# Routing of the last two tiles from rows without norm, in a hybrid decoder layer on one Trainium2 core

## The chip, the cores and the metric

One core of a Trainium2 chip runs the whole layer in one launch. The metric is the device time of one execution in microseconds, as a median over runs. Engines are named as the profile names them: PE (TensorE), PEld (its weight loads), DVE (VectorE), ACT (ScalarE), POOL (GpSimd) and SP (the queue that issues most DMAs).

## The reference, cut to what matters

```python
x = layer_norm(DN_ALPHA * x + merged @ w_out, ln1_g, ln1_b)          # 1024 tokens, 1024 wide, f32
moe = hierarchical_moe(x, ...)
x = layer_norm(DN_ALPHA * x + moe, ln2_g, ln2_b)

def layer_norm(x, g, b):
    mu = jnp.mean(xf, axis=-1, keepdims=True)
    var = jnp.mean(jnp.square(xf - mu), axis=-1, keepdims=True)
    return (xf - mu) * lax.rsqrt(var + LN_EPS) * g + b

def hierarchical_moe(x, w_rg, b_rg, w_re, b_re, ...):
    glog = xt @ w_rg + b_rg                       # 4 groups: the best one is taken
    elog = xt @ w_re + b_re                       # 32 experts: the best two of the group
    weights = gw * softmax(top_v)
    ...                                           # SwiGLU of the two experts, weighted sum
```

Ahead of this stand the input projection, a gated linear recurrence, sliding-window attention and the mixing of their two branches into `merged`.

## The kernel before

Four stages follow each other: attention with its projections, the recurrence, **mixing** (branches, `w_out`, first norm, routing) and the **experts** with the last norm. The change touches mixing alone.

Products that must be exact are three matmuls of split operands (`mm3`, lines 100 to 104). `mixing` runs 32 main steps, each in two halves, so 64 **ticks**. For each half of the tokens, 8 steps `branch(half, jt)` make `merged`, and 8 steps `project(b, i, c)` make half `c` (512 columns) of the `w_out` rows of tile `i` (128 tokens). Tile 6 is steps 28 and 29, tile 7 steps 30 and 31: its last half is ticks 62 and 63. A tick issues its half of the main step on PE, then what `self.at(tick, ...)` put on its list (line 879), then the step's `post`, then the late stages (line 885). The block stands in `all_order()`: each engine, SP's queue included, takes its instructions in exactly this order, and waits in it.

`post` of `project` (lines 815 to 822) adds the residual on DVE (L818) and its statistics (L819); after the second half `stats` (L896, L678, and the power on POOL, L679) gives mean and inverse deviation, and `norm` (line 826) runs two ticks later: `scale` is four DVE instructions per tile (L903, L904), then `store` (L842) writes the tile twice to DRAM, to `x1d` for the gathers and to `zd`, the running sum. The router works on batches of two tiles, at the tick distances in `BATCHES` (line 915): `turn` transposes a normed tile on PE (L931) and copies it (L933); `logits` multiplies by `w_r` (L940, copy with bias L941); `choose` (late) transposes the logits back (L956) and finds the best group and experts on DVE (L946 to L988); `place` (late) ranks the tokens with matmuls (L996, L998) and makes slot rows (L1002 to L1018); `enter` (late) adds them to the table of slots (L1025). All logits and ranks lie in one PSUM bank, `pa`. `warm` (line 110) issues matmuls whose result nobody reads, `WARM` (line 117) says after which ticks.

`slots` (line 1030) turns the table into row indices (L1038), starts the first two gathers of expert rows from `x1d` on POOL (L1064), splits three weight pieces and counts the fullest expert (L1050). `overflow` loads that count on every engine and branches past a loop (L1354, L1355). Then `moe` walks 384 weight **pieces** of 512 KB: 12 per expert.

Weights come by `fetch` (line 1093) on SP's queue: up to `NRAW` = 29 pieces before the experts begin (10 of them in ticks 48 to 60, 4 each after ticks 62 and 63, then 2 per tick), one per piece used after that. They live in a ring of 36 buffers (`q4`), and fetch n waits until fetch n-8 has landed (lines 1106 and 1111). At the end `final` reads all of `zd` back (L1287), behind the last weights on the same queue, and the last norm runs on ACT, DVE and POOL.

Of the kernel before, what the change touches and what calls it, by code (L numbers as in the profile page):

```python
# [5 lines left out]
F32 = mybir.dt.float32  # L6
# [54 lines left out]
class Builder:  # L61
# [679 lines left out]
    def mixing(self):  # L741
# [4 lines left out]
        self.wr = self.tile([128, 8, 36], F32, "wr", 1)  # L746
        self.br = self.tile([36, 1], F32, "br", 1)

        def constants():
# [53 lines left out]
        def project(b, i, c):  # L803
# [11 lines left out]
            def post():  # L815
                t, st = u[i]
                cs = slice(c * 512, c * 512 + 512)
                nc.vector.scalar_tensor_tensor(t[:, cs], xr[i][:, cs], ALPHA, ps, op0=ALU.mult, op1=ALU.add)  # L818
                nc.vector.bn_stats(st[:, c], t[:, cs])  # L819
                if c == 1:  # L820
                    mv = self.stats(st, LN_EPS)
                    self.at(2 * b + 2, lambda: norm(2 * b + 2, i, t, mv), True)

            return post

        def norm(b, i, t, mv):
            for c in range(2):
                self.scale(t, mv, g1, b1, c)
            self.at(b + 2 * (i < 7), lambda: store(i, t))
            batch = next(g for g in self.BATCHES if i in g[0])  # L830
            if i == batch[0][0]:
                self.batch = self.router(batch[0])
            for n, d in enumerate(batch[1]):
                fn = self.batch[n]
                if n < 2:
                    self.at(b + d, lambda fn=fn: fn(i, t))
                elif i == batch[0][-1]:
                    self.late_stages.setdefault(b + d, []).append(fn)
# [53 lines left out]

# [21 lines left out]

    BATCHES = ((0, 1), (4, 5, 6, 10, 14)), ((2, 3), (4, 5, 6, 10, 14)), ((4, 5), (2, 3, 4, 6, 7)), ((6, 7), (1, 2, 2, 3, 4))

    def router(self, batch):
# [7 lines left out]

        def turn(i, x1):
            V["xT", i] = []
            for j in range(2):
# [3 lines left out]
                xT = self.tile([128, 4, 128], F32, "rxT", 2)  # L932
                nc.scalar.copy(xT, ps)  # L933
                V["xT", i].append(xT)

        def logits(i, _):
            lg = self.pa[0:36, 0:128]
            for j, xT in enumerate(V.pop(("xT", i))):
                for k in range(4):
                    nc.tensor.matmul(lg, self.wr[:, 4 * j + k], xT[:, k], start=j + k == 0, stop=j == 1 and k == 3)  # L940
            nc.scalar.activation(lT[:, i - batch[0]], lg, AF.Identity, bias=self.br)  # L941

        def first_max(vals, w, nm, ix):

            mx = t((n, 1), nm + "m")
            vec.tensor_reduce(mx, vals, axis=AX.X, op=ALU.max)  # L946
            c = t((n, w), nm + "c")
            for k in range(n):
                vec.scalar_tensor_tensor(c[:, k], vals[:, k], mx[:, k], low[:, 0:w], op0=ALU.is_ge, op1=ALU.mult)
            vec.tensor_reduce(ix, c, axis=AX.X, op=ALU.min)  # L950
            return mx

        def choose():
            l = self.pa[:, 128:128 + 36 * n].rearrange("p (n c) -> p n c", n=n)
            for k in range(n):
                nc.tensor.transpose(l[:, k], lT[:, k], self.c("ident")[0:36, 0:36])  # L956
            gl, el = l[:, :, 0:4], l[:, :, 4:36]
            gi = t((n, 1), "gi")
            gm = first_max(gl, 4, "g", gi)
            em, ge, gs, d = t((n, 32), "em"), t((n, 4), "ge"), t((n, 1), "gs"), t((n, 1), "dd")  # L960
            for k in range(n):
                vec.tensor_scalar(em[:, k], self.c("group"), gi[:, k], -3.0e38, op0=ALU.not_equal, op1=ALU.mult)
            vec.tensor_sub(ge, gl, gm.to_broadcast([128, n, 4]))
            nc.scalar.activation(ge, ge, AF.Exp)
            vec.tensor_add(em, em, el)
            eid = self.eid[:, batch[0]:batch[0] + n]
            oh = t((n, 2, 32), "oh")
            ms = []
            for j in range(2):
                ms.append(first_max(em, 32, "ab"[j], eid[:, :, j:j + 1]))  # L970
                for k in range(n):
                    vec.tensor_scalar(oh[:, k, j], low, eid[:, k, j:j + 1], None, op0=ALU.is_equal)
                for k in range(n if j == 0 else 0):
                    vec.scalar_tensor_tensor(em[:, k], oh[:, k, 0], -3.0e38, em[:, k], op0=ALU.mult, op1=ALU.add)
            asg = t((n, 32), "asg")
# [3 lines left out]
            sums = [self.asum]  # L979
            for k in range(n):  # L980
# [8 lines left out]
            V["r"] = asg, oh, sums, gs, d  # L989

# [470 lines left out]
def arrays(inputs):  # L1461
# [11 lines left out]
        "ln1_g": f["ln1_g"][0],  # L1473
        "ln1_b": f["ln1_b"][0],
        "w_r": np.concatenate([f["router_group_w"][0], f["router_expert_w"][0]], axis=1),
        "b_r": np.concatenate([f["router_group_b"][0], f["router_expert_b"][0]]),
# [21 lines left out]
```

## Time and profile before

| | before |
|---|---|
| median of 3 runs | 1424.0 us (1423.0 to 1429.07) |
| the profiled execution | 1423.78 us |
| its span, first to last instruction | 1421.9 us |
| PE busy | 1359.1 us, 96% |
| DVE, ACT, POOL busy | 1058.2, 792.3, 239.6 us |
| DMA moved | 327.68 MB, mean 230 GB/s |

The span begins at 0 in all views. PE is busy for most of it, but with 122 instructions of `warm` among it, and the experts begin only after the routing of the last tile: the first transposes of gathered rows stand at 788.47, the last product with `w_out` starts before 763.9. The mean granted clock of TensorE is 0.986.

### The profile page before, as it was taken

The page shows a single profiled execution, that of the slowest core. Times are in us where ns is not written, and L with a number is a line of the kernel's source. Part 1 is how long each engine was busy: PE and PEld are TensorE (multiplying, and loading weights), DVE is VectorE, ACT ScalarE, POOL GpSimd, SP SyncE. Part 2 cuts the span into 40 slices and gives each one's busy share as a digit, 9 for nine tenths or more (in the row PEclk, how much of TensorE's full clock was granted, in tenths as well). Part 3 has the DMA queues.
Part 4 walks back from the last instruction along what each step waited for, and adds up shares of the span by engine and source line. Part 5 has one row for each costly group of instructions (what it writes and reads, how often), then busy time and mean ns, then how long its engine had stood idle before and what let it go on. Part 6 is the DMA issues. An engine that isn't in the chain of part 4 may idle for free. (4 is left out here: it accounts for less than half of the span.)

```text
span 1421.9 us, 20450 instructions
## 1 busy us (share of the span) xinstructions
PE 1359.1 (96%) x7162; PEld 1128.3 (79%) x7162; DVE 1058.2 (74%) x1654; ACT 792.3 (56%) x1282; POOL 239.6 (17%) x160
## 2 busy tenths in 40 slices
PE   7999999999999999999998999999999999999844
PEld 5888899988888888788787888888888888888721
DVE  4268977876666764857747889999999999999635
ACT  4367555434444442412201778888888888888533
POOL 0001221210010000410001112222222222222123
PEclk9999999999999999999999999999999999999967
DMA  6124223253334323774557899999999999999972
GB/s 254 56 89 156 88 92 105 67 173 116 126 108 136 111 88 103 240 252 137 174 195 277 314 361 369 370 359 349 360 349 359 357 359 360 360 359 361 370 264 95
DMA packets 142554, 327.68 MB, mean 230 GB/s; under 512 B 18614, under 2 KB 59702, under 8 KB 142448
## 3 DMA queue, kind: packets, MB, share of 16 engines
q1 hardware_dynamic: 132800, 308.78, 60.4%
q0 software_dynamic: 9648, 17.57, 4.8%
q8 instruction: 57, 0.93, 0.3%
q14 instruction: 49, 0.40, 0.1%
HBM read 291.43 MB, written 52.43 MB: 242 GB/s over the span
## 5 line engine op out<-in xcount | busy, mean ns | idle before, releaser
L98 DVE TENSOR_TENSOR el<-er,eh 128x1024 fp32r<-128x1024 f32 x368 | 436.5, 1221 | 53.7 <-ACT eh L97 38.1
L97 ACT CAST eh<-er 128x1024 fp32r<-128x1024 f32 x368 | 368.9, 1053 | 100.6 <-PE mm L103 83.5
L102 PE MATMUL mm<-xh,wh 128*128 128x512 f32 x480 | 198.3, 413 | 8.3 <-ACT wh L97 7.3
L102 PE MATMUL mm<-eh,xh 128*128 128x512 f32 x496 | 196.4, 396 | 0.0
L103 PE MATMUL mm<-el,xh 128*128 128x512 f32 x496 | 196.2, 395 | 0.0
L104 PE MATMUL mm<-eh,xl 128*128 128x512 f32 x496 | 196.1, 395 | 0.0
L103 PE MATMUL mm<-xl,wh 128*128 128x512 f32 x480 | 188.4, 393 | 0.8 <-DVE xl L98 0.8
L104 PE MATMUL mm<-xh,wl 128*128 128x512 f32 x480 | 189.0, 394 | 0.0
L104 PEld LDWEIGHTS mm<-eh,xl 128*128 128x128 f32 x496 | 93.2, 188 | 22.6
L103 PEld LDWEIGHTS mm<-el,xh 128*128 128x128 f32 x496 | 93.2, 188 | 22.3
L102 PEld LDWEIGHTS mm<-eh,xh 128*128 128x128 f32 x496 | 93.2, 188 | 22.3
L102 PEld LDWEIGHTS mm<-xh,wh 128*128 128x128 f32 x480 | 91.1, 190 | 24.2 <-ACT wh L97 7.3
L104 PEld LDWEIGHTS mm<-xh,wl 128*128 128x128 f32 x480 | 90.6, 189 | 20.6 <-DVE wl L98 0.8
L1064 POOL DMA_INDIRECT xg<-x1d,gi x32 | 58.1, 1814 | 279.3 <-PE pb L1127 236.3
L103 PEld LDWEIGHTS mm<-xl,wh 128*128 128x128 f32 x480 | 91.1, 190 | 16.0 <-DVE xl L98 1.4
L102 PE MATMUL mm<-eh,hth 128*128 128x512 f32 x240 | 100.2, 418 | 0.0
L1068 POOL DMA_INDIRECT zd<-y,gi x29 | 69.9, 2411 | 156.5 <-ACT y L1218 156.5
L104 PE MATMUL mm<-eh,htl 128*128 128x512 f32 x240 | 94.8, 395 | 0.0
L103 PE MATMUL mm<-el,hth 128*128 128x512 f32 x240 | 94.8, 395 | 0.0
L102 PE MATMUL mm<-wh,xh 128*128 128x256 f32 x256 | 73.1, 285 | 0.0
L104 PE MATMUL mm<-wh,xl 128*128 128x256 f32 x256 | 72.4, 283 | 0.0
L103 PE MATMUL mm<-wl,xh 128*128 128x256 f32 x256 | 72.4, 283 | 0.0
(257 smaller groups left out, 2566.6 us busy)
## 6 DMA issues: line engine op xcount, KB each, us to landing
er<-w_g SPq DMA_DIRECT2D x128, 512.0 KB, 12.5
er<-w_u SPq DMA_DIRECT2D x128, 512.0 KB, 12.5
er<-w_d SPq DMA_DIRECT2D x128, 512.0 KB, 12.0
wr<-w_in SPq DMA_DIRECT2D x38, 512.0 KB, 4.4
gated<-st SPq DMA_DIRECT2D x32, 256.0 KB, 2.1
st<-gated SPq DMA_DIRECT2D x32, 256.0 KB, 2.7
xr<-xt SPq DMA_DIRECT2D x8, 512.0 KB, 7.6
wab<-w_a SPq DMA_DIRECT2D x16, 256.0 KB, 3.7
```

The source lines that it names most:

```text
L97: self.nc.scalar.copy(hi, src)
L98: (eng or self.nc.vector).tensor_sub(lo, src, hi.bitcast(F32))
L102: mm(out, lh, rh, start=start, stop=False)
L103: mm(out, lh, rl, start=False, stop=False)
L104: mm(out, ll, rh, start=False, stop=stop)
L1064: self.nc.gpsimd.indirect_dma_start(to, None, rows, bass.IndirectOffsetOnAxis(ap=self.column(self.gi, e), axis=0), bounds_check=T - 1, oob ...
L1068: self.nc.gpsimd.indirect_dma_start(self.zd, bass.IndirectOffsetOnAxis(ap=idx, axis=0), y, None, bounds_check=T - 1, oob_is_err=False, com ...
```

## The change

- `fold`, at tick 20, makes router weights that take rows without norm: `w_r` times the norm's gain, less its column mean, in `gwr`; and `shift`, the norm's bias through `w_r` plus `b_r`. It is DVE work with one matmul between (its column sums). Two small loads are new.
- Tiles 6 and 7 go through `raw` instead of `norm`. A half tile is transposed as soon as its own half of `w_out` is there, so the first half of tile 7 is transposed and multiplied inside ticks 62 and 63. The inverse deviation and the shift come in at the start of `choose`, in one DVE instruction (`l2`).
- Tile 6 is chosen alone at tick 62, tile 7 alone at the end; `place` and `enter` still take both.
- Tile 6 keeps its norm on DVE; that of tile 7 is one ACT instruction and four on POOL, and its `store` follows in `raw`.
- The batch of tiles 4 and 5 is one tick earlier throughout (`enter` now at tick 62, ahead of the last half of `w_out`).
- 8 fetches are issued in tick 63 before its `post`; the other 11 follow the loop, behind the `store` of tile 7. Fillers: 3, 14 and 7, in `raw`.

```diff
-    WARM = {63: 11, 65: 5, 66: 14, 67: 5}
...
         def constants():
...
+            nc.sync.dma_start(gb, self.a["ln1_gb"])
+            self.shift = self.tile([128, 36], F32, "wshift", 1)
+            nc.sync.dma_start(self.shift, self.a["b_r"].partition_broadcast(128))
+
+        def fold():
+            vec = nc.vector
+            self.gwr = self.tile([128, 8, 36], F32, "gwr", 1)
+            work = self.tile([128, 512], F32, "hh", 2)
+            bwr = work[:, 0:288].rearrange("p (k c) -> p k c", k=8)
+            sums = work[:, 288:360].rearrange("p (j c) -> p j c", j=2)
+            for j, w in enumerate((self.gwr, bwr)):
+                vec.tensor_mul(w, self.wr, gb[:, j, :, None].to_broadcast([128, 8, 36]))
+                vec.tensor_reduce(sums[:, j], w.rearrange("p k c -> p c k"), axis=AX.X, op=ALU.add)
+            ps = self.pa[:, 0:72]
+            nc.tensor.matmul(ps, self.c("ones"), work[:, 288:360], start=True, stop=True)
+            for k in range(8):
+                vec.scalar_tensor_tensor(self.gwr[:, k], ps[:, 0:36], -1.0 / D, self.gwr[:, k], op0=ALU.mult, op1=ALU.add)
+            vec.tensor_add(self.shift, ps[:, 36:72], self.shift)
...
-                if c == 1:
+                if i >= 6:
+                    raw(2 * b + 2, i, t, st, c)
+                elif c == 1:
...
+        def raw(b, i, t, st, c):
+            if i == 6 and c == 0:
+                self.batch = self.router((6, 7))
+            turn, logits, choose, place, enter = self.batch
+            if c == 0:
+                self.at(b, lambda: turn(i, t, (0,)), True)
+                if i == 7:
+                    self.at(b + 1, lambda: logits(i, (0,), self.gwr))
+                return
+            if i == 6:
+                self.at(b, lambda: turn(i, t, (1,)), True)
+                mv = self.stats(st, LN_EPS)
+                self.at(b + 1, lambda: logits(i, (0, 1), self.gwr), True)
+                self.at(b + 1, lambda: [self.scale(t, mv, g1, b1, c) for c in range(2)])
+                self.at(b + 2, lambda: choose(0, 1, mv))
+                self.at(b + 3, lambda: store(i, t), True)
+                return
+            turn(i, t, (1,))
+            mv = self.stats(st, LN_EPS)
+            nm = self.tile([128, 1], F32, "lnm", 1)
+            nc.vector.scalar_tensor_tensor(nm, mv[:, 0:1], -1.0, mv[:, 1:2], op0=ALU.mult, op1=ALU.mult)
+            self.warm(3)
+            logits(i, (1,), self.gwr)
+            nc.scalar.activation(t, t, AF.Identity, scale=mv[:, 1:2], bias=nm)
+            for c in range(2):
+                cs = slice(c * 512, c * 512 + 512)
+                nc.gpsimd.tensor_mul(t[:, cs], t[:, cs], g1[:, cs])
+                nc.gpsimd.tensor_add(t[:, cs], t[:, cs], b1[:, cs])
+            choose(1, 2, mv)
+            self.warm(14)
+            place()
+            store(i, t)
+            self.warm(7)
+            enter()
...
+        self.at(20, fold)
...
+            if tick == 2 * len(main) - 1:
+                for _ in range(8):
+                    self.fetch(True)
             if post:
                 post()
...
-            self.warm(self.WARM.get(tick, 0))
             tick += 1
-            if tick >= 2 * len(main) - 1:
-                for _ in range(4 if tick < 2 * len(main) + 1 else 2):
-                    self.fetch(True)
+        for _ in range(self.NRAW):
+            self.fetch(True)
...
-    BATCHES = ((0, 1), (4, 5, 6, 10, 14)), ((2, 3), (4, 5, 6, 10, 14)), ((4, 5), (2, 3, 4, 6, 7)), ((6, 7), (1, 2, 2, 3, 4))
+    BATCHES = ((0, 1), (4, 5, 6, 10, 14)), ((2, 3), (4, 5, 6, 10, 14)), ((4, 5), (1, 2, 3, 5, 6))
...
-        def choose():
+        def choose(k0=0, k1=n, mv=None):
...
+            if mv is not None:
+                l2 = t((1, 36), "l2")
+                vec.scalar_tensor_tensor(l2[:, 0], l[:, 0], mv[:, 1:2], self.shift, op0=ALU.mult, op1=ALU.add)
+                l = l2
```

`turn` and `logits` get the halves to work on, `choose` and `first_max` the number of tiles.

## Rows read from the trace of the kernel before

**Rows 1.** Busy time by engine of one stretch of the experts, clock, DMA share, GB/s.
```profile
1000.00:1300.00 300.00, 300.00 (x1391) 244.36 (x1391) 272.47 (x267) 246.22 (x301) 72.36 (x34) 1.00 0.99 358
```
**Rows 2.** SP's waits from 1000 to 1200: us in total, times, longest.
```profile
SPq L1105 <- DMA er<-w_u: 53.1, 43, 3.4
```
**Rows 3.** Timeline at the end of the experts: start, us, what [idle before <-releaser].
```profile
1369.69 16.62 PE L1165 MATMUL mm<-er,xh 128*128 128x512 f32 x32 [23.13 <-ACT xh L1136]
1366.50 1.06 ACT L1296 ACTIVATE w<-z 128x1024 f32<-128x1024 f32 x1 [25.57 <-DMA z<-zd]
```
**Rows 4.** Timeline at tick 20, PE and DVE.
```profile
616.57 0.39 PE L104 MATMUL mm<-h,ml 128*128 128x512 f32 x1
618.68 0.75 DVE L904 SCALAR_TENSOR_TENSOR u<-u,lmv,ln_b 128x512 f32<-128x512 f32 x1
```
**Rows 5.** Timeline, DVE: an instruction over 64 columns.
```profile
774.88 0.22 DVE L965 TENSOR_TENSOR rem<-rem,pa 128x64 f32<-128x64 f32 x1
```
**Rows 6.** PE after a pause at the end: its timeline row, and the clock of 5 us.
```profile
1395.10 0.80 PE L1149 MATMUL pb<-const,hh 128*128 128x128 f32 x4 [3.64 <-DVE fv L678]
...
1395.00:1400.00 5.00, 4.90 (x11) 2.46 (x12) 4.19 (x8) 1.86 (x5) 2.90 (x2) 0.66 0.49 197
```
**Rows 7.** Timeline, PE in the last ticks.
```profile
745.77 1.94 PE L940 MATMUL pa<-rxT,wr 128*36 128x128 f32 x16
759.94 0.41 PE L996 MATMUL pa<-rasg,const 128*128 128x32 f32 x2 [0.51 <-ACT rlT L941]
```
**Rows 8.** Timeline, DVE from tile 6's second half to the row indices.
```profile
745.88 0.69 DVE L818 SCALAR_TENSOR_TENSOR u<-xr,mm 128x512 f32<-128x512 f32 x1 [4.92 <-PE mm L104]
751.04 0.17 DVE L946 TENSOR_REDUCE rgm<-pa 128x2 f32<-128x8 f32 x1
756.16 0.68 DVE L818 SCALAR_TENSOR_TENSOR u<-xr,mm 128x512 f32<-128x512 f32 x1
763.91 0.69 DVE L818 SCALAR_TENSOR_TENSOR u<-xr,mm 128x512 f32<-128x512 f32 x1 [0.74 <-PE mm L104]
768.30 0.75 DVE L904 SCALAR_TENSOR_TENSOR u<-u,lmv,ln_b 128x512 f32<-128x512 f32 x1
773.68 0.17 DVE L946 TENSOR_REDUCE rgm<-pa 128x2 f32<-128x8 f32 x1 [4.63 <-PE pa L956]
778.79 0.41 DVE L1002 TENSOR_SCALAR rpay<-roh,const 128x64 f32<-128x64 f32 x2
780.95 0.87 DVE L1018 TENSOR_SCALAR rat<-const,rank 128x128 f32<-128x128 f32 x4
782.43 0.19 DVE L1038 TENSOR_SCALAR gi<-tb 128x32 int32<-128x32 f32 x1 [0.61 <-PE tb L1025]
```
**Rows 9.** Timeline, POOL, and a DVE instruction that starts beside it.
```profile
765.90 0.91 POOL L679 TENSOR_TENSOR lmv<-lmv,mhalf 128x1 f32<-128x1 f32 x1 [17.12 <-DVE lmv L678]
579.40 2.40 POOL L98 TENSOR_TENSOR l<-wo,h 128x1024 fp32r<-128x1024 f32 x1 [3.94 <-ACT h L97]
580.10 2.24 DVE L797 TENSOR_TENSOR st<-st,st 128x512 f32<-128x512 f32 x1
```
**Rows 10.** SP's timeline, and its longest wait in the branch.
```profile
769.08 0.33 SPq L842 DMA_DIRECT2D x1d<-u  x1
791.39 3.65 SPq L1102 DMA_DIRECT2D er<-w_d  x4
...
SPq L1355 <- SPq L1355: 3.7, 1, 3.7
```
**Rows 11.** DMA from 784 to 796, GB/s in 40 slices of 0.3 us.
```profile
GB/s 423 382 423 423 396 382 301 259 233 164 110 109 138 68 123 164 68 27 68 55 41 0 27 14 55 110 68 68 218 273 355 396 355 369 300 300 328 273 300 300
```
**Rows 12.** Timeline of the first gather and its reader; all gathers' time to landing.
```profile
783.51 1.46 POOL L1064 DMA_INDIRECT xg<-x1d,gi  x1 [14.90 <-DVE tw L1039]
788.47 1.07 PE L1127 MATMUL pb<-const,xg 128*128 128x128 f32 x8 [1.33 <-DMA xg<-x1d,gi]
...
DMA to landing us min/median/max: 4.3/8.1/9.7
```

More of the change, by code (lines that the diff above doesn't have):

```diff
@@ L747, in mixing @@
         self.br = self.tile([36, 1], F32, "br", 1)
+        gb = self.tile([128, 2, 8], F32, "gb", 1)
         def constants():
@@ L828, in norm @@
                 self.scale(t, mv, g1, b1, c)
-            self.at(b + 2 * (i < 7), lambda: store(i, t))
+            self.at(b + 2, lambda: store(i, t))
             batch = next(g for g in self.BATCHES if i in g[0])
@@ L924, in router, with turn @@
         lT = self.tile([36, n, 128], F32, "rlT", 1)
-        def turn(i, x1):
-            V["xT", i] = []
-            for j in range(2):
+        def turn(i, x1, js=(0, 1)):
+            for j in js:
                 ps = self.bank("pb", (128, 4, 128))
@@ L931, in turn, with logits, first_max @@
                     nc.tensor.transpose(ps[:, k], x1[:, (4 * j + k) * 128:(4 * j + k + 1) * 128], self.c("ident"))
[L932 to L936, printed above, removed]
+                V["xT", i, j] = self.tile([128, 4, 128], F32, "rxT", 2)
+                nc.scalar.copy(V["xT", i, j], ps)
+        def logits(i, js=(0, 1), w=None):
             lg = self.pa[0:36, 0:128]
-            for j, xT in enumerate(V.pop(("xT", i))):
+            for j in js:
+                xT = V.pop(("xT", i, j))
                 for k in range(4):
[L940 to L945, printed above, removed]
+                    nc.tensor.matmul(lg, (self.wr if w is None else w)[:, 4 * j + k], xT[:, k], start=j + k == 0, stop=j == 1 and k == 3)
+            if js[-1] == 1:
+                if w is None:
+                    nc.scalar.activation(lT[:, i - batch[0]], lg, AF.Identity, bias=self.br)
+                else:
+                    nc.scalar.copy(lT[:, i - batch[0]], lg)
+        def first_max(vals, m, w, nm, ix):
+            mx = t((n, 1), nm + "m")[:, 0:m]
             vec.tensor_reduce(mx, vals, axis=AX.X, op=ALU.max)
-            c = t((n, w), nm + "c")
-            for k in range(n):
+            c = t((n, w), nm + "c")[:, 0:m]
+            for k in range(m):
                 vec.scalar_tensor_tensor(c[:, k], vals[:, k], mx[:, k], low[:, 0:w], op0=ALU.is_ge, op1=ALU.mult)
@@ L951, in first_max @@
             return mx
-        def choose():
+        def choose(k0=0, k1=n, mv=None):
+            if k0 == 0:
+                V["r"] = t((n, 32), "asg"), t((n, 2, 32), "oh"), [self.asum], t((n, 1), "gs"), t((n, 1), "dd")
+            m, ks = k1 - k0, slice(k0, k1)
             l = self.pa[:, 128:128 + 36 * n].rearrange("p (n c) -> p n c", n=n)
-            for k in range(n):
+            for k in range(k0, k1):
                 nc.tensor.transpose(l[:, k], lT[:, k], self.c("ident")[0:36, 0:36])
+            l = l[:, ks]
+            if mv is not None:
+                l2 = t((1, 36), "l2")
+                vec.scalar_tensor_tensor(l2[:, 0], l[:, 0], mv[:, 1:2], self.shift, op0=ALU.mult, op1=ALU.add)
+                l = l2
+            asg, oh, sums, gs, d = V["r"]
+            asg, oh, gs, d = asg[:, ks], oh[:, ks], gs[:, ks], d[:, ks]
@@ L957, in choose @@
             gl, el = l[:, :, 0:4], l[:, :, 4:36]
[L958 to L961, printed above, removed]
+            gi = t((n, 1), "gi")[:, 0:m]
+            gm = first_max(gl, m, 4, "g", gi)
+            em, ge = t((n, 32), "em")[:, 0:m], t((n, 4), "ge")[:, 0:m]
+            for k in range(m):
                 vec.tensor_scalar(em[:, k], self.c("group"), gi[:, k], -3.0e38, op0=ALU.not_equal, op1=ALU.mult)
-            vec.tensor_sub(ge, gl, gm.to_broadcast([128, n, 4]))
+            vec.tensor_sub(ge, gl, gm.to_broadcast([128, m, 4]))
@@ L964, in choose @@
             nc.scalar.activation(ge, ge, AF.Exp)
             vec.tensor_add(em, em, el)
-            eid = self.eid[:, batch[0]:batch[0] + n]
-            oh = t((n, 2, 32), "oh")
+            eid = self.eid[:, batch[k0]:batch[k0] + m]
             ms = []
             for j in range(2):
-                ms.append(first_max(em, 32, "ab"[j], eid[:, :, j:j + 1]))
-                for k in range(n):
+                ms.append(first_max(em, m, 32, "ab"[j], eid[:, :, j:j + 1]))
+                for k in range(m):
@@ L972, in choose @@
                     vec.tensor_scalar(oh[:, k, j], low, eid[:, k, j:j + 1], None, op0=ALU.is_equal)
-                for k in range(n if j == 0 else 0):
+                for k in range(m if j == 0 else 0):
                     vec.scalar_tensor_tensor(em[:, k], oh[:, k, 0], -3.0e38, em[:, k], op0=ALU.mult, op1=ALU.add)
-            asg = t((n, 32), "asg")
             vec.tensor_add(asg, oh[:, :, 0], oh[:, :, 1])
@@ L978, in choose @@
             nc.scalar.activation(d, d, AF.Exp)
-            sums = [self.asum]
-            for k in range(n):
+            for k in range(m):
                 new = t(32, "sum", 6)
@@ L1474, in arrays @@
         "ln1_b": f["ln1_b"][0],
+        "ln1_gb": np.ascontiguousarray(np.stack([f[k][0].reshape(8, 128).T for k in ("ln1_g", "ln1_b")], axis=1)),
         "w_r": np.concatenate([f["router_group_w"][0], f["router_expert_w"][0]], axis=1),
```

5 lines of the change are left out of this document (3 added, 2 removed).

## The prediction

> **What bounds the kernel now.** First the windows: in the experts PE is never idle, and the DMA engines are busy 0.99 of the time [rows 1], so either could set the pace. SP's own waits decide between them: from 1000 on it waits above all for weight pieces issued earlier to land (53.1 us behind one of the three matrices alone [rows 2]), not for PE to free buffers. The weight stream is the slower of the two; the 29 pieces fetched ahead hide that until near the end. There the bill comes: PE stands still for 23.13 us before the last expert's products, behind ACT, and ACT has waited 25.57 us for the first rows of `zd`, which are loaded behind the last weights on the same queue [rows 3]. So the end follows the weight stream. What counts is when the stream's last long run begins and what it leaves unused after that; an earlier or later PE only uses up or adds to the 23.13 us.
>
> That run begins with the store of tile 7 at 769.08 [rows 10]: 11 fetches stand behind it on SP's queue. They run at full rate until about 785.8; then a lull until 793.0 [rows 11]. In these 7.2 us the 24 slices add up to 0.83 MB, some 2.0 us of full rate, so 5.2 us are lost. It isn't PE that ends the lull: SP is held for 3.7 us behind its own branch and issues the next piece at 791.39 [rows 10].
>
> Before all that, in mixing, PE sets the pace; a wait there shifts everything after it.
>
> **The change part by part, as a shift of the store of tile 7 and then of the stream.** Times are those of the profiled execution, 1423.78 us (span 1421.9, so 1.9 lie around it); the median is 1424.0, 0.2 more.
>
> *Fold, at tick 20.* The list of that tick is the norm of tile 0 (put first by the `post` of tile 0), then `fold`. PE's matmul of column sums stands behind the first half of main step 10, whose last matmul starts at 616.57; the next would start at 616.80. DVE is in the norm of tile 0 until 618.68 + 0.75 = 619.43 [rows 4]. Only then come two products over 288 elements and two sums over them. No row has that size: 64 columns take 0.22 [rows 5] and 512 take 0.69 [rows 8]; on the line between them 288 take 0.45, four of them 1.8 (ends 0.9 and 2.8). So PE gets its matmul at 621.2 and goes on at 621.5 after two short instructions: 4.7 us late (3.8 to 5.7). PE has nothing to put into this pause, and the filler matmuls are elsewhere. The pause of 4.3 us also touches the clock: after a pause of 3.64 us at the end of the kernel the granted clock fell from 2.4 to 1.2 GHz and was 0.66 on average over 5 us, which loses 0.34 x 5 = 1.7 us [rows 6]. The other end is 0, if it doesn't fall; I take 1.6, from that nearest row. Together **+6.3 us** (3.8 to 7.4). The eight corrections after the matmul cost DVE about 2 us more, and DVE, idle before its next `post`, catches up. The two small loads at tick 12 are two more issues on a queue that isn't late: nothing.
>
> *DVE in the last ticks.* Between the second half of tile 6 and that of tile 7, DVE has now: residual, statistics and mean 1.85 (from 763.91 to just ahead of POOL's power at 765.90 [rows 8, 9]); the choice of tiles 4 and 5, 756.16 - 751.04 = 5.1; the norm of tile 6, 4 x 0.75 = 3.0; the first half of tile 7, 1.4; `place` of 4 and 5, from 778.79 to 780.95 + 0.87, 3.0; and, new, the choice of tile 6 alone. Of a pair's 5.1 the per-tile instructions fall away once, some 1.6, and `l2` adds 0.2: 3.7. The sum is 18.1. It also begins later than 745.88: the logits of tile 5 (1.94 [rows 7]) and half a transpose (0.4) now stand on PE ahead of that half: 748.3. So the residual of tile 7's last half starts at 766.4 in place of 763.91: **+2.5 us** (1.5 to 4). PE comes to nearly the same: it has `enter` of tiles 4 and 5 before its last half and must wait there for DVE's slot rows. The bank `pa` adds waits of the kind of the 0.51 us [rows 7]; the choice of tile 6 writes it behind DVE's last read of the ranks, at about that time.
>
> *The norm of tile 7.* Counted from that residual, s. Before: norm on DVE to 768.30 + 0.75, store at s + 5.2. After: second half transposed at s + 0.9 to s + 1.5, copied on ACT to s + 2.1, half the logits, their copy done at about s + 3.6. The one ACT instruction of the norm stands behind that copy in ACT's order: 1.06 for 1024 columns [rows 3], to s + 4.7. Then four instructions on POOL over 512 columns, each half of 2.40 [rows 9]: 4.8, with their starts and DVE in between 5.1. Store at s + 9.8: **+4.6 us** (3.5 to 6.5). Behind this store wait 11 fetches on SP, and on POOL the two memsets and the gathers.
>
> *The lull.* The 8 fetches of tick 63 don't depend on that store and are through before it. From the store on SP has the same work as before, some 17 us of transfers. But now PE and the gathers begin inside it, and SP passes its branch before the stream is empty. The lull shrinks; it doesn't vanish, if the eight semaphore waits at L1355 want every piece landed: the thinning tail of the stream (0.9 lost of 1.7), the eight waits and the issue (0.7), and from issue to full rate 793.0 - 791.39 = 1.6, less some gather. About 2.9 lost in place of 5.2: **-2.3 us** (-5.2 if SP need not wait; 0 if its code comes late because the DMA engines are full).
>
> *The choice of tile 7.* Before, from the residual to the indices: 782.43 - 763.91 = 18.5. After: no norm ahead of the transposes, 4.4 less; half the logits, 1.0 less; one tile less in the choice, 1.4 less: about 11.6, so 6.9 gained. This is the largest term of the change, but it frees PE, not the stream. Part of it also goes back: a DVE instruction with both inputs in SBUF that starts beside a POOL instruction takes 2.24 in place of 0.69, to the POOL instruction's end and its own half microsecond [rows 9]. The choice of tile 7 and the four POOL instructions fall into the same 5 us, and ten of its DVE instructions are of that kind; I put 4 us on it (0 to 5). Then the gather starts at 766.4 + 6.3 + 11.6 + 4 + 0.9 = 789.2, in a full stream, where gathers take 8.1 to land [rows 12]; the first transposes come at 797.4, 9 us later than 788.47, which the 23.13 us swallow. The Trainium skill, "SBUF — State Buffer", section "Who interferes with whom", says the same of this pair of engines and more: whoever starts first holds the shared port for its whole instruction and the other is blocked. The POOL row agrees with the first half (2.40 beside a waiting DVE); by the second a short DVE instruction would also hold up the next POOL one, by 0.2 us each, some 0.6 us more on the store's path, and the sum would be 1435.5.
>
> **Sum.** 6.3 + 2.5 + 4.6 - 2.3 = +11.1 us: 1423.78 + 11.1 = 1434.9, said as **1435 us**, +0.8%. Its bounds: the lows without the clock, 3.8 + 1.5 + 3.5 - 5.2 = +3.6, the highs 7.4 + 4.0 + 6.5 - 0 = +17.9; not all at once, so 1430 to 1440.
>
> **Rivals.**
> *Slower, further out.* SP's code after the branch, 3.7 us in a quiet queue [rows 10], takes twice that in a full one, and the lull stays as long as it was; POOL is slower beside DVE. Against it: SP is through the branch some 3 us before the stream ends. 11.1 + 2.3 + 2 gives 1439. Chance 0.12.
> *No change to be measured.* The wait in `fold` is hidden, or the stream has more slack than the waits tell: without the 6.3 us, 1428.6. For it: in mixing the DMA engines have room. Against it: the order of tick 20 is fixed, and nothing else can start on PE. Chance 0.17.
> *Faster.* The choice, not the weights, sets the end: then 6.9 - 2.5 = 4.4 us are gained at the indices, 1419.4. It decides only if the stream has that much in hand, that is, if the 23.13 us before the last expert come from ACT's order and not from the load it waits for, and if DVE's sums of `fold` are ready by 616.80. For it: PE never idles before that. Against it: rows 2 and 3, and the blocked DVE. Chance 0.08.
>
> **How the numbers follow.** Forecast 0.63, the slower rival 0.12, no change 0.17, faster 0.08. About 0.5%, 7 us, is what a measurement of this kernel can tell from no change: 1417 to 1431. The forecast's low end just touches it, so faster 0.08, within 0.5% 0.19, slower 0.73. The range reaches from inside the no-change case to above the slower rival, 1426 to 1440.
>
> **What would show it.** After tick 20: PE idle for some 4 us before a matmul out of line with the rest, between the first and second half of main step 10, and a stretch below full clock after it. The residual of tile 7's last half 8 to 9 us later than 763.91, with DVE busy up to it. Store of tile 7 near 782.5, behind four POOL instructions of 1.2 us. Stretched DVE instructions beside them. First gathered rows transposed at 795 or later. A short lull of the DMA engines near 802. At the end the pause of PE before the last expert some 2 us longer than 23.13, since PE starts 9 later and the stream 11. The forecast is wrong if the pause in tick 20 is under 2 us, or if the load of `zd` isn't later by what the stream lost.

## The result and the profile after

| | before | after |
|---|---|---|
| median | 1424.3 us (1423.0 to 1429.07) | 1438.1 us (1437.55 to 1438.84) |
| ratio after to before, 95% interval | | 1.0094 (1.0076 to 1.0113) |
| profiled execution, its span | 1423.78, 1421.9 us | 1438.03, 1436.3 us |
| PE, DVE, ACT, POOL busy | 1359.1, 1058.2, 792.3, 239.6 us | 1364.3, 1071.2, 802.3, 204.5 us |
| mean granted clock | 0.986 | 0.979 |

The changed kernel is slower by 13.8 us (0.9%, the interval of the ratio lies above 1); +11.1 was forecast. In the profiled executions the spans differ by 14.4 us. The views below follow the prediction's steps. All are timelines (start, us, what, idle time before it and its releaser) unless another view is named.

**The fold.** PE around tick 20, after:

```profile
618.37 0.39 PE L104 MATMUL mm<-h,ml 128*128 128x512 f32 x1
623.33 0.70 PE L769 MATMUL pa<-hh,const 128*128 128x72 f32 x2 [4.58 <-DVE hh L767]
623.78 0.77 PE L102 MATMUL mm<-h,mh 128*128 128x512 f32 x1
...
627.74 0.39 PE L102 MATMUL mm<-h,mh 128*128 128x512 f32 x1
```

618.37 answers to the last product of the first half at 616.57 [rows 4]. It is 1.80 late before the fold has done anything; where that comes from is the subject of three runs below. The column sums wait 4.58 us for DVE. The next product starts at 623.78, not 616.80: 6.98 late, so 5.18 are the fold's. Then nine products stand 0.44 apart on average (3.96 us in all) in place of the 0.23 on either side, as PE runs at 1.2 in place of 2.4 GHz there (the granted clock is 0.53 on average from 622 to 628): 9 x 0.23 = 2.07, so 1.9 are lost. DVE shows what PE waited for:

```profile
620.45 0.75 DVE L965 SCALAR_TENSOR_TENSOR u<-u,lmv,ln_b 128x512 f32<-128x512 f32 x1
621.12 0.45 DVE L766 TENSOR_TENSOR gwr<-wr,gb 128x288 f32<-128x288 f32 x1
...
622.64 0.64 DVE L767 TENSOR_REDUCE hh<-hh 128x36 f32<-128x288 f32 x1
624.07 0.91 DVE L771 SCALAR_TENSOR_TENSOR gwr<-pa,gwr 128x36 f32<-128x36 f32 x8 [0.80 <-PE pa L769]
```

The end of the norm of tile 0, then the products and sums, as the order of the list has them: the norm to 621.2, two products and two sums (one of each is shown), PE's release at 623.3.

**The last ticks and the choice of tile 7.** DVE, after. The first two rows are from the choice of tile 6, the third is the residual of tile 7's last half, the others are from the choice of tile 7:

```profile
771.45 0.25 DVE L1028 SCALAR_TENSOR_TENSOR rl<-pa,lmv,wshift 128x36 f32<-128x36 f32 x1
...
775.11 0.19 DVE L1049 TENSOR_TENSOR rasg<-roh 128x32 f32<-128x32 f32 x1
...
775.51 0.68 DVE L837 SCALAR_TENSOR_TENSOR u<-xr,mm 128x512 f32<-128x512 f32 x1
...
779.28 0.25 DVE L1028 SCALAR_TENSOR_TENSOR rl<-pa,lmv,wshift 128x36 f32<-128x36 f32 x1 [1.04 <-PE pa L1024]
...
780.22 1.25 DVE L1037 TENSOR_SCALAR rem<-const,rgi 128x32 f32<-128x32 f32 x1
...
781.73 0.19 DVE L1010 TENSOR_REDUCE ram<-rem 128x1 f32<-128x32 f32 x1
781.95 0.92 DVE L1013 SCALAR_TENSOR_TENSOR rac<-rem,ram,const 128x32 f32<-128x32 f32 x1
...
783.13 0.95 DVE L1046 TENSOR_SCALAR roh<-const,eid 128x32 f32<-128x32 f32 x1
...
784.56 0.92 DVE L1013 SCALAR_TENSOR_TENSOR rbc<-rem,rbm,const 128x32 f32<-128x32 f32 x1
...
785.74 1.51 DVE L1046 TENSOR_SCALAR roh<-const,eid 128x32 f32<-128x32 f32 x1
787.28 0.19 DVE L1049 TENSOR_TENSOR rasg<-roh 128x32 f32<-128x32 f32 x1
```

The residual comes 11.6 after the 763.91 of before [rows 8]. From L1028 to the start of L1049 the choice of tile 6 takes 3.66 (771.45 to 775.11), that of tile 7 takes 8.00 (779.28 to 787.28) for the same work. Five instructions are stretched: 1.25, 0.95 and 1.51 in place of 0.24 (tile 6's three TENSOR_SCALARs), 0.92 twice in place of 0.25. Together 4.33 us, all of the difference. POOL, after, is what they stand beside:

```profile
780.16 1.27 POOL L874 TENSOR_TENSOR u<-u,ln_g 128x512 f32<-128x512 f32 x1 [2.12 <-ACT u L871]
781.51 1.31 POOL L875 TENSOR_TENSOR u<-u,ln_b 128x512 f32<-128x512 f32 x1
...
784.12 1.31 POOL L875 TENSOR_TENSOR u<-u,ln_b 128x512 f32<-128x512 f32 x1
785.37 1.84 POOL L1106 MEMSET xg<- 128x1024 f32 x2
```

Each stretched instruction ends 0.04 us or so after a POOL one: 780.22 + 1.25 = 781.47 beside 780.16 + 1.27 = 781.43, and so on to 787.25 beside 787.21. The memset row holds two, and the instruction at 785.74 ends with the second. The reduction at 781.73, in the middle of a POOL instruction, takes its usual 0.19.

**Store, lull and start of the experts.** PE, after:

```profile
787.53 0.63 PE L1067 MATMUL pa<-rasg,const 128*128 128x32 f32 x2 [4.59 <-DVE rasg L1049]
...
801.66 1.86 PE L1198 MATMUL pb<-const,xg 128*128 128x128 f32 x8 [4.39 <-DMA xg<-x1d,gi]
```

The store of tile 7 on SP's queue, after:

```profile
785.46 0.33 SPq L901 DMA_DIRECT2D x1d<-u  x1
```

SP's instructions at the line of its branch, after (count, durations in ns, first and last start):

```profile
L1426 SPq EVENT_SEMAPHORE  x8: 17/17/17, 803.4 to 808.2; - x8
L1426 SPq COMPARE_BRANCH  x1: 50/50/50, 797.1 to 797.1; - x1
```

The GB/s from 800 to 812 in 40 slices of 0.3 us, after:

```profile
GB/s 369 410 451 396 328 328 314 369 300 410 396 410 410 287 260 246 191 164 206 164 137 164 191 205 178 150 178 109 68 14 0 177 150 205 259 341 355 410 437 410
```

The store of tile 7 is at 785.46, 16.4 after the 769.08 of [rows 10]. SP passes its branch at 797.1 and goes on at 803.4, 6.3 later (3.7 before [rows 10]). Its eight waits then take until 808.2. The lull is shallower: from 803.9 to 810.5 the 22 slices add up to 1.11 MB, 2.7 us at full rate (410 GB/s), so 3.9 of 6.6 us are lost, where before lost 5.2 of 7.2 [rows 11]: 1.3 less. The first gathered rows are transposed at 801.66, 13.2 later than in [rows 12].

**The end.** The last expert's first products, and the first rows of the last norm on ACT, after:

```profile
1384.05 16.37 PE L1236 MATMUL mm<-er,xh 128*128 128x512 f32 x32 [23.14 <-ACT xh L1207]
1380.85 1.06 ACT L1367 ACTIVATE w<-z 128x1024 f32<-128x1024 f32 x1 [27.15 <-DMA z<-zd]
```

Both come 14.4 later than in [rows 3], and the pause is the same 23.1.

### The profile page after: what moved, and what is told of

It is laid out like the page before. It is cut to its first block, busy times and chain, and to the rows that moved or that the text cites. A ratio compares the mean times of both kernels' runs of the same rounds, so it can differ in the third digit from the quotient of the medians.

```text
span 1436.3 us, 20481 instructions
## 1 busy us (share of the span) xinstructions
PE 1364.3 (95%) x7142; PEld 1132.1 (79%) x7142; DVE 1071.2 (75%) x1677; ACT 802.3 (56%) x1285; POOL 204.5 (14%) x164
## 5 line engine op out<-in xcount | busy, mean ns | idle before, releaser
L97 ACT CAST eh<-er 128x1024 fp32r<-128x1024 f32 x368 | 377.5, 1052 | 90.0 <-PE mm L103 55.2
L1139 POOL DMA_INDIRECT zd<-y,gi x29 | 53.7, 1853 | 211.0 <-ACT y L1289 195.1
L1135 POOL DMA_INDIRECT xg<-x1d,gi x32 | 35.4, 1107 | 261.0 <-PE pb L1198 237.8
```

The source lines that it names most:

```text
L97: self.nc.scalar.copy(hi, src)
L1135: self.nc.gpsimd.indirect_dma_start(to, None, rows, bass.IndirectOffsetOnAxis(ap=self.column(self.gi, e), axis=0), bounds_check=T - 1, oob ...
L1139: self.nc.gpsimd.indirect_dma_start(self.zd, bass.IndirectOffsetOnAxis(ap=idx, axis=0), y, None, bounds_check=T - 1, oob_is_err=False, com ...
```

## The experiments

Each is compared with runs of the kernel before on the same chip. "Ahead of the fold" means up to 616.57 of [rows 4], or the same product in another kernel.

**1. The fold in two ticks** (the changed kernel otherwise):

```diff
-            work = self.tile([128, 512], F32, "hh", 2)
+            work = self.fwork = self.tile([128, 512], F32, "hh", 2)
...
+        def fold_rest():
+            vec, work = nc.vector, self.fwork
             ps = self.pa[:, 0:72]
...
         self.at(20, fold)
+        self.at(22, fold_rest)
```

> The changed kernel with the matmul of fold and the eight corrections two ticks after its sums, so that PE finds them ready. Theory (PE's wait of 4.6 us in tick 20 and the half clock after it, 7.1 us in all, shift everything behind): about 1431 us, no pause of PE over 1 us near 620, clock 1.0 there. Rival (the wait was swallowed by a later one, since DVE sets the pace in the last ticks): 1437 to 1438.

Measured: 1432.26 us (1430.36 to 1435.99), ratio 1.0053 (1.0037 to 1.007): 5.8 us less than the change. The windows (busy us of PE, PEld, DVE, ACT and POOL with their instructions, clock, DMA share, GB/s) of the changed kernel, then of this one, then a row of this one's PE timeline:

```profile
610.00:640.00 30.00, 25.18 (x106) 20.15 (x105) 17.86 (x36) 5.18 (x6) 4.39 (x3) 0.89 0.48 162
```

```profile
610.00:640.00 30.00, 30.00 (x145) 24.79 (x144) 20.64 (x39) 5.55 (x8) 4.40 (x3) 1.00 0.59 193
```

```profile
598.98 0.79 PE L104 MATMUL mm<-h,l 128*128 128x512 f32 x1 [2.60 <-DVE l L98]
```

The pause and the half clock are gone; so they were the fold's, and without them the end comes 5.8 earlier by the medians, of the 7.1 that they took in the changed kernel's profile. The last row shows that this execution, at 1435.99 the longest of the four, had a pause of its own ahead of the fold with a half clock after it; a comparison of this single trace with another would be off by that.

**2. Tile 7's norm on DVE**, right behind its statistics:

```diff
-            nm = self.tile([128, 1], F32, "lnm", 1)
-            nc.vector.scalar_tensor_tensor(nm, mv[:, 0:1], -1.0, mv[:, 1:2], op0=ALU.mult, op1=ALU.mult)
+            for c in range(2):
+                self.scale(t, mv, g1, b1, c)
             self.warm(3)
             logits(i, (1,), self.gwr)
-            nc.scalar.activation(t, t, AF.Identity, scale=mv[:, 1:2], bias=nm)
-            for c in range(2):
-                cs = slice(c * 512, c * 512 + 512)
-                nc.gpsimd.tensor_mul(t[:, cs], t[:, cs], g1[:, cs])
-                nc.gpsimd.tensor_add(t[:, cs], t[:, cs], b1[:, cs])
```

> The changed kernel with the norm of tile 7 back on DVE, four instructions right after its statistics, ahead of its logits. Theory (the store of tile 7 starts the last run of the weight stream, and DVE's choice is stretched beside POOL): store 4.5 to 5 us earlier counted from the residual of the last half, choice of tile 7 on DVE back to about 3.9 us from 8.1, end 4 to 5 us earlier, about 1433.5 us. Rival (the choice sets the end, and the norm on DVE puts it off by 1.2 us): 1439 us.

Measured: 1434.66 us (1434.31 to 1435.44), ratio 1.0077 (1.006 to 1.0093): 3.4 less than the change. DVE, then the store on SP's queue, then SP's instructions at its branch:

```profile
772.83 0.68 DVE L837 SCALAR_TENSOR_TENSOR u<-xr,mm 128x512 f32<-128x512 f32 x1
...
777.88 0.25 DVE L1023 SCALAR_TENSOR_TENSOR rl<-pa,lmv,wshift 128x36 f32<-128x36 f32 x1
...
781.54 0.19 DVE L1044 TENSOR_TENSOR rasg<-roh 128x32 f32<-128x32 f32 x1
```

```profile
777.99 0.33 SPq L896 DMA_DIRECT2D x1d<-u  x1
```

```profile
L1421 SPq EVENT_SEMAPHORE  x8: 17/17/17, 797.1 to 800.3; - x8
L1421 SPq COMPARE_BRANCH  x1: 50/50/50, 791.1 to 791.1; - x1
```

The store stands 5.16 behind the residual in place of 9.95. The choice takes 3.66 to the start of L1044, as that of tile 6 did, and none of its instructions is stretched. So POOL did both: it made the norm longer and held DVE up. How much of the 4.8 us that the store gained arrived at the end is less clear. By the medians it is 3.4. But from the residual to the end of the span it is 659.5 here and 660.5 to 660.8 in three profiles of the change (experiments 9 and 10 are the other two), so 1.0 to 1.3 less; the rest of the difference between the profiles lies ahead of the residual, where the two kernels are the same. The first transposes of gathered rows, at 797.08, stand 24.25 behind the residual, 1.9 less than after the change. The eight waits end 27.5 behind the residual, 32.7 after the change, but the SP code is no faster (6.0 us from branch to first wait).

**3. 40 more matmuls on PE, nobody reads them**, in the middle of expert 24 (of the changed kernel):

```diff
+            if i == at[24, "w_u", 1]:
+                spare = self.bank("pb", (128, 4, 128))
+                for _ in range(40):
+                    nc_ = self.nc
+                    nc_.tensor.matmul(spare[:, 0], self.c("ident"), self.c("ident"), start=True, stop=True)
```

> The changed kernel with 40 more matmuls that nobody reads on PE, some 9.6 us, in the middle of expert 24. Theory (the weight stream sets the end): 1438 us within 1 us, and PE's pause before the last expert falls from 23.1 to about 13.5 us. Rival (PE sets the pace of the experts): 9.6 us more, 1447.7 us.

Measured: 1440.26 us (1438.64 to 1441.11), ratio 1.0112 (1.0096 to 1.0129), 2.2 more than the change, with intervals that overlap. The added line (durations in ns, first and last start), then the pause before the last expert:

```profile
L1340 PE MATMUL pb<-const x80: 272/275/275, 1243.4 to 1252.3; 128*128 128x128 f32 x80
```

```profile
1386.20 16.86 PE L1236 MATMUL mm<-er,xh 128*128 128x512 f32 x32 [14.05 <-ACT xh L1207]
```

PE works on them for 9.1 us, and the pause shrinks by 9.1 (23.14 to 14.05): what PE loses as late as this is taken out of the pause. Its own prediction, no change within 1 us, missed by 1.2. In this execution the store stands at 785.21, 0.25 earlier than after the change, and the span ends 653.2 behind it, not 650.8; SP's code took 6.6 us. The fetch of the 41st piece stands at 824.3, 2.3 later than after the change and over 400 us ahead of the added matmuls: the 2.2 us are there by then, so they aren't the price of the matmuls. What caused them stays open.

**4. The kernel before with 12 fetches, not 8, ahead of tile 7's store:**

```diff
-    NRAW = 29
+    NRAW = 28
...
-                for _ in range(4 if tick < 2 * len(main) + 1 else 2):
+                for _ in range(8 if tick == 2 * len(main) else 4 if tick < 2 * len(main) else 2):
```

> The kernel before with 4 of the 10 last fetches put ahead of the store of tile 7, so that they run in the 4 us in which the DMA engines are idle before that store; 28 pieces ahead as before. Theory (in the kernel before, the lull after the 28 pieces is ended by SP's branch and the choice ahead of it, not by the pieces): the pieces are there some 4 us earlier, the lull is longer by that, 1424 us within 1.5. Rival (only the volume of the stream counts): 4 us less, 1420 us.

Measured: 1424.9 us (1422.47 to 1430.38), ratio 1.0006 (0.9991 to 1.0022). No change. The window from 784 to 796, which has 0.64 and 212 GB/s in the kernel before, here, and then the first issue after it:

```profile
784.00:796.00 12.00, 11.70 (x77) 10.76 (x76) 7.86 (x11) 6.34 (x7) 4.17 (x3) 0.90 0.35 105
```

```profile
792.52 3.79 SPq L1102 DMA_DIRECT2D er<-w_d  x4
```

The transfers that ran early leave the DMA engines idle later, since the next issue comes when SP is through its branch. So it isn't the position of these fetches in the queue that counts; what is left is when the routing lets SP, and PE, go on.

**5. Both repairs at once** (the diffs of 1 and 2):

> The changed kernel with both edits, the matmul of fold two ticks later and the norm of tile 7 on DVE. Theory (both waits lie one behind the other on the way to the store of tile 7): their gains add up, 5.8 to 7.1 and 3.4 off 1438.1: about 1428 us; what is left over the kernel before is the residual of tile 7's last half, 2.7 us late behind the choice of tile 6. Rival (the lull behind the pieces fetched ahead swallows one of them): 1431 us or more.

Measured: 1426.55 us (1424.96 to 1430.77), ratio 1.0018 (1.0005 to 1.0031); neither gain swallows the other (5.8 and 3.4 alone, 11.6 together, by the medians; the 2.4 above their sum are less than runs of one kernel differ by, 1424.96 to 1430.77 here). 2.9 us over the kernel before are left, about the +2.7 of the last ticks.

**6. The fifth, with tiles 6 and 7 chosen together at the end:**

```diff
-                self.at(b + 2, lambda: choose(0, 1, mv))
+                self.mv6 = mv
...
-            choose(1, 2, mv)
+            choose(0, 2, (self.mv6, mv))
...
```

> As e5_fold_and_norm, and tiles 6 and 7 chosen together at the end. Theory (the choice of tile 6 alone, 3.9 us on DVE, keeps the residual of tile 7's last half waiting): residual and store 2.5 to 3 us earlier, the last choice 1.5 us longer, indices some 1 us earlier, about 1426 us. Rival (choosing tile 6 early shortens the way to the gather and with it the end): 1.5 us more than e5_fold_and_norm.

Measured: 1428.31 us (1427.05 to 1430.95), ratio 1.0029 (1.0017 to 1.0041), 1.8 more than the fifth, with times that overlap (1424.96 to 1430.77 there). The residual of tile 7's last half, first in the fifth with PE's last product ahead of it, then in this one:

```profile
767.03 0.39 PE L104 MATMUL mm<-h,ml 128*128 128x512 f32 x1
...
768.03 0.68 DVE L840 SCALAR_TENSOR_TENSOR u<-xr,mm 128x512 f32<-128x512 f32 x1
```

```profile
768.42 0.39 PE L104 MATMUL mm<-h,ml 128*128 128x512 f32 x1
768.85 0.69 DVE L840 SCALAR_TENSOR_TENSOR u<-xr,mm 128x512 f32<-128x512 f32 x1 [3.42 <-PE mm L104]
```

The theory fell: with the choice of tile 6 gone from that place DVE is idle for 3.42 and waits for PE. In the fifth DVE started 0.61 after PE's product ended, here 0.04 after: all that the choice cost was 0.6. The choice of two tiles is longer: the row indices come 15.5 after that residual (784.32), in the fifth 13.7 (781.77). That this costs 1.8 at the end isn't shown. This execution has a pause of PE near 599 us, as that of experiment 1, and is 1.40 late at tile 6's second half (751.23, in the fifth 749.83), ahead of anything that the edit touches. Counted from there, the store comes 0.6 earlier than in the fifth, the indices 1.1 later, the first transposes 0.2 later, and the span ends 0.5 earlier.

**7. The kernel before, 31 pieces ahead and 12 of them ahead of the store** (the diff of 4, with `NRAW = 31`):

> The kernel before with 31 pieces fetched ahead in place of 28, 12 of them ahead of the store of tile 7 in place of 8. Theory (the end is set by how many bytes of the stream are through when the experts begin, and the lull before that is idle): three pieces of 1.46 us less to fetch behind it, about 1420 us. Rival (the beginning of the experts on PE sets the end): 1424 us.

Measured: 1421.21 us (1418.41 to 1427.42), ratio 0.9984 (0.997 to 0.9997), faster than both kernels by a little. The last expert, and the window from 1000 to 1300:

```profile
1371.02 14.00 PE L1165 MATMUL mm<-er,xh 128*128 128x512 f32 x32 [1.46 <-ACT xh L1136]
```

```profile
1000.00:1300.00 300.00, 293.12 (x1347) 234.82 (x1346) 267.17 (x257) 241.84 (x290) 57.91 (x33) 1.00 0.99 361
```

The pause of 23.1 is down to 1.46, and only 2.4 us are gained by the medians (this profile, at 1425.14, is the second longest of the ten): PE now loses 6.9 us from 1000 to 1300, 16 times 0.4 behind DVE's `hh`, where it lost none [rows 1]. The pause is where PE's slack collects; it isn't a sum that can be had.

**8. The sixth with the same depth:**

> As e6_pair_choice, with 31 pieces ahead in place of 29, 12 of them ahead of the store of tile 7 in place of 8. Theory: the two pieces and the 4 us in which the DMA engines are idle ahead of the store come to 3 to 5 us less than e6_pair_choice, about 1422 us, and the experts begin no later. Rival (a ring that full keeps the splits of the first pieces waiting, or the gather lands late in the full stream): no less than e6_pair_choice.

Measured: 1428.55 us (1425.07 to 1431.2), ratio 1.0032 (1.0022 to 1.0043): nothing gained over the sixth. SP at its branch, in it:

```profile
L1426 SPq EVENT_SEMAPHORE  x8: 17/17/17, 796.9 to 797.5; - x8
L1426 SPq COMPARE_BRANCH  x1: 50/50/50, 786.8 to 786.8; - x1
```

The branch comes early, at 786.8, while weights are still landing. SP's code takes 10.1 us to arrive, 5.5 in the sixth. Whether that alone ate the gain was not tried by itself.

**9 to 11. The change twice more, and the kernel before once more**, for the 1.80 us ahead of the fold. From 20 to 30 us the changed kernel's first profile shows a clock of 0.83, that of before 1.00:

```profile
20.00:30.00 10.00, 8.24 (x28) 6.13 (x27) 4.72 (x4) 4.97 (x8) 0.00 (x0) 0.83 0.38 126
```

> The changed kernel as it is, profiled once more. In the first profile of it the last product ahead of the fold came 1.80 us later than before (618.37 against 616.57), since the granted clock was 0.83 between 20 and 30 us, far ahead of anything the change touches. Theory: such a start falls into some executions of any kernel and is not part of the change. Then a profile without it is possible here: clock 1.00 in 20 to 30 us, the last product ahead of the fold at 616.6, and the execution near 1436.3. Rival: the start belongs to the changed kernel; then clock 0.83 and 618.4 again, near 1438.1. The pause at the fold is 4.6 us in either case.

> The changed kernel as it is, a third profile: the same two expectations as of the second (theory: the clock between 20 and 30 us is 1.00 in some execution, the last product ahead of the fold then at 616.6; rival: 0.83 and 618.4 in each). Three profiles alike, all with the slow start, speak for the rival; one without it is enough against it.

> The kernel before as it is, profiled once more. By the theory the start at half clock may show here too (0.83 between 20 and 30 us, the last product ahead of tick 20 at 618.4); by the rival it may not: clock 1.00 and 616.6, as in its first profile. The rest as in its first profile: store of tile 7 at 769.1 or 1.8 later, pause before the last expert 23.1.

Measured, one execution each: 1437.03, 1436.82 and 1426.02 us (spans 1435.3, 1435.1, 1424.1), all three with a clock of 1.00 from 20 to 30 us. The third profile of the change:

```profile
616.73 0.39 PE L104 MATMUL mm<-h,ml 128*128 128x512 f32 x1
621.70 0.71 PE L769 MATMUL pa<-hh,const 128*128 128x72 f32 x2 [4.59 <-DVE hh L767]
622.15 0.78 PE L102 MATMUL mm<-h,mh 128*128 128x512 f32 x1
```

It reaches the fold 0.16 late, not 1.80. So the slow start isn't part of the change; the profiles of 3, 7 and 8 have it as well, two of them of kernels without the pause, one of them the kernel before but for the fetches. The second profile of the change was 1.52 late there with its start at full clock, so the start is not the only source of such a shift. The pause at the fold is 4.6 us in all three. The second profile of the kernel before has the store of tile 7 0.8 later than the first (769.89) and the end of the span 2.2 later (1424.1), so what lies behind the store differs by 1.4 between two executions of that one kernel.

## Why the prediction was right

The 1435 us, its range of 1426 to 1440 and its sign hold, and 1438.1 lies nearer to the upper end. Of the four terms the first three came as described; the step from the store to the end was met by its size, not by its reason. The terms in three profiles of the changed kernel against the first of before, each worked out from the marks named in it (before in the table; after 618.37, 654.39, 775.51, 785.46 and 1436.3 in the first, 618.09, 653.69, 774.83, 784.77 and 1435.3 in the second, 616.73, 653.27, 774.47, 784.41 and 1435.1 in the third):

| term | predicted | 1st | 2nd | 3rd |
|---|---|---|---|---|
| ahead of the fold (last product, 616.57) | 0 | 1.8 | 1.5 | 0.2 |
| fold (to the DVE residual at 645.45, less the line above) | 6.3 | 7.1 | 6.7 | 7.7 |
| last ticks (from there to 763.91) | 2.5 | 2.7 | 2.7 | 2.7 |
| norm of tile 7 (from there to the store, 769.08) | 4.6 | 4.8 | 4.8 | 4.8 |
| stream (from the store to the end of the span, 1421.9) | -2.3 | -2.0 | -2.3 | -2.1 |
| sum, spans | 11.1 | 14.4 | 13.4 | 13.2 |

*Fold.* The order of the list and the place of the pause were read rightly. It was mis-sized by 0.4 to 1.4: a column sum over 288 elements took 0.64, not the 0.45 of the line between contiguous rows (0.38 for the two), and the half clock took 1.9, 1.7 and 2.4 us in the three profiles (in the second ten products from 623.08 to 627.05, in the third twelve from 622.15 to 627.30, at 0.23 each without it), where the 1.6 was taken from another pause. Experiment 1 gives 5.8 by the medians. The eight corrections took 0.91, not 2, and cost nothing.

*Last ticks.* +2.5 predicted, +2.7 in each profile, and the sum that gave it held in its parts: in the first profile DVE has 18.2 us of work from tile 6's second half (757.33) to the residual of tile 7's last half (775.51), said 18.1, and 757.33 less the 8.94 that lie ahead of it is 748.39, said 748.3. The choice of tile 6 took 4.1 of it, not 3.7. That PE comes to nearly the same held too: in experiment 6, where DVE is rid of that choice, only 0.6 are gained before DVE waits for PE.

*Norm of tile 7.* The store stands at s + 9.95, said 9.8. The Trainium skill, "SBUF — State Buffer", section "Who interferes with whom", was weighed in the prediction with 0.6 us for short DVE instructions that hold POOL up; the four POOL instructions took 5.27 from first start to last end, 0.2 over the 5.1 of the sum, so nearer to the sum without it.

*The choice, and POOL beside it.* The block cost 4.3, said 4, but not by the kind of instruction named: five were stretched, not ten, and three of these are TENSOR_SCALARs with one input of 128 x 32, one of them beside two memsets, which read nothing. The same section says that `tensor_scalar` can take both ports and `tensor_reduce` never does, and the rows agree: 1.25 for the one, 0.19 for the other, both beside POOL's products. Experiment 2 shows the same choice without POOL at its full speed.

*The gain of the choice that frees PE.* The first transposes came at 801.66, not 797.4: 1.8 were there before the fold, 0.8 more came with it, 0.2 with the last ticks. Of the rest, 1.0 lies between `rasg` and the row indices, which took 5.3 (787.28 to 792.57) where the kernel before took 4.3; there PE had just waited 4.59 for `rasg`, and its granted clock is 0.67 on average from 785 to 795. The pause before the last expert, said to grow by 2, stayed at 23.14 (why is told below).

*The lull.* It shrank by 1.3, to 3.9, where 2.9 had been forecast: the eight waits run from 803.4 to 808.2, so SP goes on only some 5 us after its code is there. In the kernel before they were over by 791.2, 0.5 after the code. Before, 10 fetches stood behind the store, not the 11 of the text (2 + 4 + 4 in [rows 10]), and 28 pieces were fetched ahead, not 29; the eleventh is new, in the run that the store holds back, and the 17 us were read from the view, so the sum doesn't move. The rival "SP's code comes late" was partly right: 6.3 in place of 3.7, though the lull still shrank. The row "stream" holds all from the store to the end, not the lull alone. Its -2.0 to -2.3 become -3.4 to -3.7 against the second profile of the kernel before, and in the kernels of experiments 1, 2, 3, 5 and 6 the same row is +2.3, +1.5, +0.4, +0.6 and +0.7. That it met the forecast so closely is luck.

*That the store sets the end.* The rows don't bear this step out. The prediction read SP's waits from 1000 on, where they are for pieces to land. Right behind the branch they are others (us in total, times, longest; before from 800 to 850, then after from 810 to 870, two rows of four each):

```profile
SPq L1105 <- PE mm L104: 26.9, 19, 2.8
SPq L1102 <- PE mm L104: 11.9, 11, 1.6
```

```profile
SPq L1176 <- PE mm L104: 25.2, 17, 2.9
SPq L1173 <- DVE el L98: 8.3, 8, 1.7
```

There SP waits for PE's products and DVE's splits, which free the buffers of the ring: by all four rows 40.7 of the 50 us before and 44.5 of the 60 after, none of it for a landing. So the stream starts at the pace of the experts, and when PE begins with them counts for it. The distances say the same. In the eleven profiles with 28 or 29 pieces ahead, the first transposes of gathered rows stand 633.4 to 636.4 ahead of the end of the span, the store of tile 7 650.5 to 655.1. And the pause before the last expert, which was to change with the store, is 22.1 to 23.9 in ten of them (23.1 in experiment 3 too, with the 9.1 of the added matmuls). Experiment 2 fits: counted from the residual its store comes 4.8 earlier, its first transposes 1.9, its end 1.0 to 1.3. So a later start of PE in the experts is not just taken out of the pause, as the prediction had it; a loss as late as that of experiment 3 is. No run moved the store or the first transposes alone, so this stands on waits and distances, not on an experiment of its own.

By this mark the 14.4 us of the first profile are 1.8 ahead of the fold, 7.1 of the fold, 2.7 of the last ticks, 1.6 from the residual to the first transposes (26.15 in place of 24.56: the shorter choice, POOL beside it, and a gather that lands later) and 1.2 behind these; the last two stand in place of the norm's 4.8 and the stream's -2.0. The total came near the forecast because the store (16.4) and the first transposes (13.2) moved by not very different amounts. Experiment 4 fits: fetches moved ahead of the store gain nothing. Deeper prefetch gained 2.4 once and nothing once. Which wait sets the time of the deeper kernel is open.

Faster (chance 0.08) didn't happen: the first transposes came 13.2 later, not earlier. But its condition, that the choice and not the weights sets the end, is nearer to these rows than the forecast's.

## What to carry to other kernels

A wait that was put ahead of PE in a hand-written order cost its whole length here, and the half clock after it; split such work over two ticks, so that the sums are done before PE comes to them (5.8 us here). Work moved from DVE to POOL to unload DVE slowed the DVE chain beside it (3.66 to 8.00 us): move it to where that chain isn't, or leave it. Before counting on one queue to set the end, read its waits over the whole way: here SP waits for landings late, and for PE and DVE right behind the branch.

## What the runs showed of the hardware that was not expected

- SP's code after its branch takes 3.7 to 4.0 us where the stream has thinned by then (before, twice, and experiments 4 and 7: 63 to 86 GB/s from the branch on), 5.4 to 6.6 where it runs on (the change, three times, and 1, 2, 3, 5, 6: 320 to 394 GB/s) and 10.1 in experiment 8, at 313 GB/s; what made it longest there is open. The other four engines have their first instruction at that line behind the branch 0.1 to 0.7 us later (before and after). The Trainium skill, "Runtime: NRT & Kernel Launch", section "Instruction fetch mechanics", says that a taken branch to code outside the pages held forces a DMA fetch before the engine goes on. SP's waits agree in kind; from 797 to 804 the instruction queues moved four packets after the change, but no row says for which engine.
- A TENSOR_SCALAR of 0.24 us beside POOL ran to the end of the POOL instruction (1.25 and 0.95), and one that began beside the first of two memsets to the end of the second (1.51).
- The pause of 4.6 us at the fold is the same in three profiles, but the half clock after it cost 1.7, 1.9 and 2.4 us.
- Three profiled executions of the changed kernel reach the last product ahead of the fold at 616.73, 618.09 and 618.37, the last of them with a clock of 0.83 from 20 to 30 us: single profiles can't be compared to better than 1.6 us without a mark ahead of the change.
